# A two-layer hybrid decoder step on one core: evacuations, attention steps and weight parts are queued by the time their own engine gets to them, and low parts by DMA are chosen by an estimate of their landing

## The chip, the cores and the metric

One core of one Trainium2 chip runs the whole program. The metric is device microseconds of one execution; each time named as a median is over the runs taken, and one execution was also profiled. Engines are called as in the profile: PE (TensorE, its matmuls), PEld (its weight loads), DVE (VectorE), ACT (ScalarE), POOL (GpSimd), SP (SyncE). Transfers run on the 16 DMA engines of the core; SP, ACT and POOL issue them.

## The reference

Two layers over 576 tokens (512 of a prompt, 8 sequences of 8 sampled tokens), width 1024, all in float32:

```python
for l in range(DEPTH):
    rq, rk, rv, rg, sq, sk, sv, mq, g_r, g_s, g_m = in_proj(x, w_in[l], pos)
    ret_o = retention(rq, rk, rv); swa_o = sink_window_attend(sq, sk, sv)
    mem_o = mem_attend(mq, mk, mv)
    ret_b = (silu(rg) * group_norm(ret_o, gn_g)) @ w_br_ret
    swa_b, mem_b = swa_o @ w_br_swa, mem_o @ w_br_mem
    merged = sigmoid(g_r) * ret_b + sigmoid(g_s) * swa_b + sigmoid(g_m) * mem_b
    x = layer_norm(ALPHA * x + merged @ w_out, ln1_g, ln1_b)
    h = square(relu(x @ w_up))
    x = layer_norm(ALPHA * x + h @ w_down, ln2_g, ln2_b)
```

## The kernel before

**Tiling.** Features lie on the partitions. The tokens are two groups, A and B, of 288. A weight *unit* is a 1024x128 piece of a weight matrix, 128x1024 in the chip (512 KB); `unit_order` lists 154 of them a layer, in the order mk, mv (memory keys and values), rk, rq, rv, rg (retention), sv, sk, sq (window attention), gr and br, mq, gs and bs, gm and bm (gates and branch outputs), wo, up, then pairs ua/ub with dh, and dn. Every float32 value is held as two fp32r parts, high and low, and a product of a unit with a group is 24 matmuls of 128x288: 8 slots, each high by high, high by low and low by high.

**Parts of a unit.** The raw unit comes by a DMA that SP issues (`fetch`, 545). `split` (551) makes the two parts: the high part is a cast on ACT or DVE. The low part is made in one of two ways: on DVE, a subtraction of 128x1024 (`T<-T,T`); or by ACT and a DMA, where ACT writes minus the high part (ACTIVATE `T<-T`) and POOL issues a DMA that adds the raw unit to it (`T<-T` by POOLq). Lines 560 and 561 choose: the DMA is taken if the unit's use lies over `FAR` = 11 us ahead and its key is none of mq, gs, bs, gm, bm. The pairs ua/ub of the MLP are seven half-width products of sums of the two units (`block`, 570; `pair_steps`, 661), as in Strassen's scheme, and `sums` (713) forms the matching sums of tokens.

**The order of the work.** All instructions are written by one Python program in the order in which it calls them; each engine runs its own in that order. `Clock` (268) holds a cost model of every engine, which runs along while the program is written; it decides the order alone, and its times are no measurements. `plan` (240) gives every unit a planned time of use. `run` (617) writes the steps of a phase; inside a product, after each 6 matmuls, `Filler.advance` (404) looks at what else may be put in: generators (`add`), which yield tiles they wait for, and single instructions put off by `later` (390). Both are put in when `ok` (399) says that their input is ready `EARLY` = 0.4 us after the planned time of PE, or earlier. `tick` (598) puts in the parts of the next unit: all of them at once, when ACT has no work ahead or the use is within `LEAD` = 13 us. `soonest` (523) takes the engine that would be done first. Evacuations of a product (`up_ev`, the closure `evac` of `pair_steps`) are written right behind its last matmul.

**The layer norms.** `norm_ev` (842) is called on each of the 8 outputs of wo or dn for a group, adds it to the residual y, and keeps running sums. `shift` (867) subtracts a mean from y (`T<-T,u` 128x1152); `half` squares and sums; `last` (887) ends the norm: two mean products on PE (`pa<-t,ones`), reciprocal root in tiles `ln` and `u`, four multiplies of y (`z = [mult(i) ...]`, 939), the affine step on ACT (`T<-T,par` 128x288, which writes the high part of the next input) and an `end` on DVE that makes the low part. wo runs all of A, then all of B, then up all of A and all of B, so that A's norm ends under B's products of wo, and B's norm under A's products of up. The start of layer 1 does the same with dn and the first products, whose mk and mv units do not depend on the norm.

All instructions are recorded with line 359, the wrapper `timed`, so rows are told apart by tiles: `T` big tiles, `u` and `t` tiles of 128x288, `pg` and `pa` PSUM banks.

Of the kernel before, what the change touches and what calls it, by code (L numbers as in the profile page):

```python
# [8 lines left out]
F32 = mybir.dt.float32  # L9
# [27 lines left out]
EARLY = 0.4  # L37
EARLY_PE = -0.8
LEAD = 13.0
FAR = 11.0  # L40
DN_SKEW = 7
START = 3
STEP = 2
# [331 lines left out]
    pass  # L375


class Filler:
    def __init__(self, clock):
        self.t = 0.0  # L380
# [6 lines left out]
        self.gens.append([gen, self.clock.now, lane])  # L387
        self.gens.sort(key=lambda r: r[2])

    def later(self, fn, wait, *aps):  # L390
        self.late.append((self.t + wait, fn, aps))

    def flush(self, upto=None):
        due = [x for x in self.late if upto is None or x[0] <= upto or self.ok(x[2])]
        self.late = [x for x in self.late if x not in due]
        for _, f, _ in due:
            f()

    def ok(self, cond):
        if isinstance(cond, float):  # L400
            return cond <= self.clock.now
        return self.clock.ready(cond) - (EARLY_PE if isinstance(cond, Pe) else EARLY) <= self.clock.now

    def advance(self, dt):
        self.t += dt
# [31 lines left out]
                self.step(rec)  # L437

    def drain(self):
        self.flush()  # L440
        while self.gens:
            busy = set()
            for rec in list(self.gens):
                if rec[2] in busy:
                    continue
                busy.add(rec[2])
                self.step(rec)


class Builder:  # L450
    def __init__(self, nc, tc, I, O, coff, pools):
        self.tc, self.I, self.O, self.coff = tc, I, O, coff
        self.clock = Clock()
        self.nc = Engines(nc, self.clock)
        self.sb, self.ps, self.dr = pools
        self.n = 0
        self.fill = Filler(self.clock)
        self.banks = []
        self.raw, self.w = {}, {}
        self.dma_next = self.split_next = 0  # L460
        self.cap = 4
        self.items = items()
        self.item = {(k, b): i for i, (u, k, b) in enumerate(self.items)}
        self.use = plan(self.items)
        self.live = {}
        self.between = iter(())
        self.fill.tick = self.tick

# [82 lines left out]
    def split(self, i):  # L551
        u, k, b = self.items[i]
        if b is not None:
            self.w[i] = self.block(u, b)
            self.live[i] = 1
            return
        raw = self.raw.pop(u)
        hi = self.tile([P, 8, P], F32R)
        lo = self.tile([P, 8, P], F32R)
        if self.use[i] - self.fill.t > FAR and k[1] not in ("mq", "gs", "bs", "gm", "bm") and u > 15 \  # L560
                and (k[1] != "dh" or k[2] == 0):
            self.nc.scalar.copy(hi, raw)
            self.nc.scalar.activation(lo, raw, AF.Copy, scale=-1.0)
            self.nc.gpsimd.dma_start(lo, raw, accum_op=ALU.add)
        else:
            self.split_into(hi, lo, raw, True)
        self.w[i] = (hi, lo)
        self.live[i] = 2

    def block(self, u, b):  # L570


        V = self.nc.vector
        ra, rb = self.raw[u - 1], self.raw[u]
# [12 lines left out]
        w = self.tile([P, 8, P], F32R)  # L587
        self.nc.scalar.copy(w[:, 0:4], src)
        if b == 5 and self.items[self.split_next][1][2] == 7:
            self.nc.scalar.activation(w[:, 4:8], src, AF.Copy, scale=-1.0)  # L590
            self.nc.gpsimd.dma_start(w[:, 4:8], src, accum_op=ALU.add)
        else:
            V.tensor_tensor(w[:, 4:8], src, w[:, 0:4].bitcast(F32), ALU.subtract)
        if b == 6:
            del self.raw[u - 1], self.raw[u], self.raw[u, "s"]
        return w[:, 0:4], w[:, 4:8]

    def tick(self):
        n, i = len(self.use), self.split_next
        if i >= n or self.use[i] > self.fill.t + LOOK:  # L600
            return
# [15 lines left out]
    def run(self, steps, cap=3):  # L617
# [5 lines left out]
        for i, (units, fn, tick) in enumerate(steps):  # L623
            while units and self.split_next <= max(units):
                self.feed()
            fn()
            for u in units:
                if last[u] == i:
# [32 lines left out]
    def pair_steps(self, key, XT, evac):  # L661


        V, S = self.nc.vector, self.nc.scalar
# [15 lines left out]
        def sub(k, a, b):  # L680
            st[k] = self.u()
            V.tensor_tensor(st[k], a, b, ALU.subtract)

        def e0():
            st["s1"] = self.u()
            S.copy(st["s1"], st["z"])

        def e1():
            sub("w", st.pop("v"), st.pop("s1"))
# [3 lines left out]

        def e3():
            sub("o", st.pop("v7"), st["y"])
            evac(1, "B", st.pop("o"))

        def e4():
            evac(0, "A", st.pop("z"))

        def e5():
            sub("o", st["w"], st.pop("x"))
            evac(1, "A", st.pop("o"))

        def e6():
            sub("o", st.pop("y"), st.pop("w"))
            evac(0, "B", st.pop("o"))
        return [step(0, lambda: (bank("z", "g"), True, e0)), step(1, lambda: (bank("v", "g"), True, e1)),
                step(2, lambda: (bank("x", "a"), True, e2)), step(3, lambda: (bank("y", "a"), True, e3)),
                step(4, lambda: (st["z"], False, e4)), step(5, lambda: (st["x"], False, e5)),  # L710
                step(6, lambda: (st["y"], False, e6))]

# [129 lines left out]
    def norm_ev(self, g, y, l, gi, eps, out, scale=None, bias=1.0):  # L842
# [24 lines left out]
        def shift():  # L867
# [4 lines left out]
            V.tensor_scalar(st["c"], pm, 4.0, None, ALU.mult)  # L872
            cb = st["c"].unsqueeze(1).to_broadcast([P, 4, n])
            self.pick(y[1], st["c"], bias=bias).tensor_tensor(y[1], y[1], cb, ALU.subtract)

        def half():
            c = st.pop("c")
# [9 lines left out]
        def last():  # L887
# [48 lines left out]
            if out is not None:  # L936
                out[g]["h"] += [self.tile([P, 4, n], F32R) for _ in range(2)]
                out[g]["l"] += [self.tile([P, 4, n], F32R) for _ in range(2)]
            z = [mult(i) for i in range(4)]
            step = 1 if out is None else STEP  # L940
            wait = ()
            for i in range(0, 4, step):
# [22 lines left out]
        def ev(m, ps):  # L965
# [22 lines left out]
            elif m > 4:  # L988
# [4 lines left out]
                if m == 7:  # L993
                    self.fill.flush()
                    self.pick(sq, st["s2"]).tensor_tensor(st["s2"], st["s2"], sq, ALU.add)
                    st["last"] = last()
                    self.fill.add(st["last"], 0)
                else:
                    self.fill.later(lambda: self.pick(sq, st["s2"], bias=bias).tensor_tensor(st["s2"], st["s2"], sq, ALU.add),
# [481 lines left out]
    def layer(self, l, X):  # L1481
# [377 lines left out]
        for q in range(2, 8):  # L1859
            H.append(self.feat_tiles(1))  # L1860
            steps = []
            for j in range(2):
                def pev(i, g, ps, j=j, q=q):
                    up_ev(2 * j + i, H[-1])(g, ps)
# [7 lines left out]
            if 2 < q < 5:  # L1872
                k = ("swk", "swv")[q - 3]
                nc.gpsimd.dma_start(self.O[k + "_c"][l], self.I[k + "_n"][l])
        del Ts, XT, X1
        H = {g: {k: [h[g][k][0] for h in H] for k in "hl"} for g in "AB"}
        if True:
# [93 lines left out]
```

## Time and profile before

| | |
|---|---|
| median of 3 runs | 2158.07 us (2150.84 to 2158.13) |
| profiled execution | 2157.69 us, its span 2155.9 us |
| granted TensorE clock, mean of the span | 0.992 |
| PE busy | 2118.5 us, 98% |
| DVE, ACT, POOL busy | 59%, 43%, 11% |
| DMA | 292.42 MB, mean 136 GB/s |

A row of a group gives busy time, and behind a bar the idle time of the engine just before. In a timeline, a row is a run of like instructions on one engine: its start, its length from the first start to the last end, and in brackets how long the engine had stood idle before the first of them and what ended that. `pg<-T,T` is the output tile and its inputs. A run of matmuls that is longer than its count of matmuls times the time of one holds gaps too. For a DMA, "to landing" runs from its issue to its last byte.

### The profile page before, as it was taken

What the parts mean: (1) busy time and instruction counts of PE and PEld (TensorE: products, weight loads), DVE (VectorE), ACT (ScalarE), POOL (GpSimd) and SP (SyncE); (2) the same over time, 40 slices, a digit from 0 to 9 for tenths busy, and PEclk for the clock granted to TensorE, in tenths of its full rate; (3) what the DMA queues carried; (4) which work ended last, traced back from release to release, by engine and by line L of the source; (5) the groups of instructions that cost most, each with busy time, mean ns of one, the idle gap of its engine ahead of it and who ended that gap; (6) DMA issues with size and microseconds to landing.
All of it is one profiled execution on the core that took longest, in us unless ns stands there. A gap on an engine that the chain in (4) does not pass through costs nothing.

```text
span 2155.9 us, 39206 instructions
## 1 busy us (share of the span) xinstructions
PE 2118.5 (98%) x16180; PEld 2058.2 (95%) x16180; DVE 1261.5 (59%) x2705; ACT 925.6 (43%) x1750; POOL 232.9 (11%) x297
## 2 busy tenths in 40 slices
PE   9999999999999999999989999999999999999997
PEld 8999999999999999999989999999999999999997
DVE  6455644456547576765745556444565565767766
ACT  4333355322256444446553333562221665444452
POOL 0111111000022000000321111000000220000012
PEclk9999999999999999999999999999999999999999
DMA  8455645434375422225895556544342854222242
GB/s 316 114 143 134 166 118 120 145 109 144 119 211 127 126 94 84 79 88 151 204 266 143 144 141 174 122 114 132 135 157 85 229 120 130 79 79 99 98 122 60
DMA packets 87618, 292.42 MB, mean 136 GB/s; under 512 B 9552, under 2 KB 19280, under 8 KB 87376
## 3 DMA queue, kind: packets, MB, share of 16 engines
q0 software_dynamic: 31408, 113.79, 24.0%
q1 hardware_dynamic: 50944, 168.27, 22.8%
q10 hardware_dynamic: 5088, 7.87, 1.1%
q8 instruction: 127, 2.08, 0.4%
q14 instruction: 51, 0.42, 0.1%
HBM read 200.89 MB, written 15.99 MB: 101 GB/s over the span
## 4 chain that ended last, share of the span: by engine, by line
PE 91%; DVE 4%; issue 2%; DMA 2%; ACT 1%; POOL 0%; SPq 0%; DVEq 0%; POOLq 0%; ACTq 0%
PE pg L359 69%; PE pa L359 23%; DVE T L359 3%; DMA T<-T 1%; ACT T L359 1%; DVE u L359 0%; DMA T<-in_wall 0%; ACT u L359 0%; DMA T<-in_memT 0%; SPq L359 0%; DVE ln L359 0%; DVE accA L359 0%; DVE s L359 0%; POOL T L359 0%; POOL rc L359 0%
## 5 line engine op out<-in xcount | busy, mean ns | idle before, releaser
L359 PE MATMUL pg<-T,T 128*128 128x288 f32 (+1 forms) x11840 | 1643.3, 297 | 19.3 <-ACT T L359 10.9
L359 PEld LDWEIGHTS pg<-T,T 128*128 128x128 f32 x11840 | 1591.4, 190 | 44.4 <-ACT T L359 17.0
L359 PE MATMUL pa<-T,T 128*128 128x288 f32 (+8 forms) x3368 | 449.5, 303 | 2.4 <-DVE u L359 2.4
L359 ACT CAST T<-T 128x1024 fp32r<-128x1024 f32 (+6 forms) x464 | 354.6, 789 | 210.1 <-DVE T L359 174.7
L359 PEld LDWEIGHTS pa<-T,T 128*128 128x128 f32 (+3 forms) x3368 | 399.7, 176 | 23.0 <-issue 9.5
L359 DVE TENSOR_TENSOR T<-T,T 128x512 fp32r<-128x512 f32 (+8 forms) x418 | 361.9, 878 | 85.2 <-ACT T L359 75.4
L359 POOL DMA_DIRECT2D T<-T x145 | 124.7, 868 | 1379.2 <-ACT T L359 1013.2
L359 ACT ACTIVATE T<-T 128x1024 fp32r<-128x1024 f32 (+2 forms) x157 | 165.3, 1054 | 10.5 <-DVE T L359 8.2
L359 ACT ACTIVATE t<-pg 128x288 f32<-128x288 f32 x128 | 52.6, 411 | 215.8 <-PE pg L359 210.5
L359 ACT ACTIVATE u<-u 128x288 f32<-128x288 f32 x200 | 89.0, 445 | 96.0 <-DVE u L359 92.0
L359 DVE TENSOR_TENSOR T<-u,T 128x288 fp32r<-128x288 f32 x160 | 72.4, 454 | 78.0 <-ACT T L359 78.0
L359 ACT COPY T<-pg 128x512 f32<-128x512 f32 (+2 forms) x44 | 20.8, 479 | 213.0 <-PE pg L359 213.0
L359 DVE TENSOR_TENSOR T<-T,pg 128x288 f32<-128x288 f32 x128 | 57.7, 451 | 75.6 <-PE pg L359 75.1
L359 ACT CAST T<-u 128x288 fp32r<-128x288 f32 x160 | 69.3, 433 | 52.6 <-DVE u L359 48.6
L359 DVE TENSOR_TENSOR T<-T,u 128x288 f32<-128x288 f32 (+2 forms) x136 | 88.1, 660 | 3.8
L359 DVE SCALAR_TENSOR_TENSOR T<-t,pg 128x288 f32<-128x288 f32 x64 | 29.0, 453 | 94.0 <-ACT t L359 76.2
L359 DVE TENSOR_TENSOR T<-T,pa 128x288 f32<-128x288 f32 (+1 forms) x92 | 52.1, 567 | 25.1 <-PE pa L359 23.7
L359 DVE TENSOR_TENSOR T<-pa,T 128x512 fp32r<-128x512 f32 (+2 forms) x48 | 24.9, 533 | 64.9 <-ACT T L359 64.7
L359 DVE SCALAR_TENSOR_TENSOR u<-t,pg 128x288 f32<-128x288 f32 x64 | 28.8, 450 | 55.8 <-PE pg L359 55.2
L359 DVE TENSOR_TENSOR u<-u,pa 128x288 f32<-128x288 f32 x72 | 32.6, 453 | 35.2 <-PE pa L359 35.0
L359 ACT CAST T<-pa 128x512 fp32r<-128x512 f32 (+2 forms) x44 | 19.4, 451 | 70.2 <-PE pa L359 66.3
L359 DVE CAST T<-T 128x1024 fp32r<-128x1024 f32 (+1 forms) x71 | 45.2, 641 | 1.0 <-DMA T<-in_wall 1.0
(164 smaller groups left out, 1095.3 us busy)
## 6 DMA issues: line engine op xcount, KB each, us to landing
T<-in_wall SPq DMA_DIRECT2D x305, 512.0 KB, 4.2
T<-T POOLq DMA_DIRECT2D x141, 512.0 KB, 5.7
T<-in_mck POOLq DMA_DIRECT2D x16, 512.0 KB, 4.4
T<-in_mcv POOLq DMA_DIRECT2D x16, 512.0 KB, 6.6
T<-in_s POOLq DMA_DIRECT2D x8, 512.0 KB, 8.2
out_state_s<-T POOLq DMA_DIRECT2D x8, 512.0 KB, 3.8
T<-in_xT SPq DMA_DIRECT2D x4, 576.0 KB, 10.4
T<-in_xT ACTq DMA_DIRECT2D x4, 576.0 KB, 6.8
```

The source lines that it names most:

```text
L359: r = f(*a, **kw)
```

## The change

- `FAR` and the list of keys go. `in_time` estimates, with the cost model, when ACT would be done, when POOL would issue, and when the bytes would land behind the DMAs already put in, and takes the DMA way if that and `MARGIN` = 1.5 us lie before the use.
- The low part on DVE and the parts of a `block` become generators (`part`, `proceed`): each is put in when the model says its engine gets to it with its input ready, at the latest before the step that uses it.
- `ok` compares readiness no longer with PE's planned time alone, but with the later of that and the time at which the engine (`On`) is free.
- In `pair_steps` the copy of the first bank (`e0`) goes to the sooner of ACT and DVE, and three of four evacuations of a pair are put off by `later` for ACT.
- In `norm_ev`, A's four final multiplies wait in the program until B's shift has been put in (`shifting`).
- `settle` empties the put-off list at the end of the pairs and in `drain`.

```diff
-FAR = 11.0
+MARGIN = 1.5
...
+class On(tuple):
+    def __new__(cls, eng, *aps):
+        r = tuple.__new__(cls, aps)
+        r.eng = eng
+        return r
...
-    def later(self, fn, wait, *aps):
-        self.late.append((self.t + wait, fn, aps))
+    def later(self, fn, wait, *aps, eng="vector"):
+        self.late.append((self.t + wait, fn, On(eng, *aps)))
...
+    def settle(self):
+        while self.late:
+            self.flush()
+
     def ok(self, cond):
         if isinstance(cond, float):
             return cond <= self.clock.now
-        return self.clock.ready(cond) - (EARLY_PE if isinstance(cond, Pe) else EARLY) <= self.clock.now
+        c = self.clock
+        if isinstance(cond, Pe):
+            return c.ready(cond) - EARLY_PE <= c.now
+        return c.ready(cond) - EARLY <= max(c.now, c.te[cond.eng] if isinstance(cond, On)
+                                            else min(c.te["vector"], c.te["scalar"]))
...
         if b is not None:
-            self.w[i] = self.block(u, b)
+            w = self.tile([P, 8, P], F32R)
+            self.w[i] = w[:, 0:4], w[:, 4:8]
+            self.part(i, self.block(w, u, b))
...
-        if self.use[i] - self.fill.t > FAR and k[1] not in ("mq", "gs", "bs", "gm", "bm") and u > 15 \
-                and (k[1] != "dh" or k[2] == 0):
+        if u > 15 and (k[1] != "dh" or k[2] == 0) and self.in_time(i, raw):
             self.nc.scalar.copy(hi, raw)
             self.nc.scalar.activation(lo, raw, AF.Copy, scale=-1.0)
             self.nc.gpsimd.dma_start(lo, raw, accum_op=ALU.add)
         else:
-            self.split_into(hi, lo, raw, True)
+            def low(raw=raw):
+                self.rounded(hi, raw)
+                yield On("vector", hi)
+                self.nc.vector.tensor_tensor(lo, raw, hi.bitcast(F32), ALU.subtract)
+            self.part(i, low())
...
+    def in_time(self, i, src):
+        c, n = self.clock, src.free_size()
+        t = max(c.te["scalar"], c.ready((src,))) + 2 * (0.19 + n / 1200.0)
+        t = max(t, c.te["gpsimd"]) + 1.04
+        t = max(t + 1.7, c.te["dma"]) + n * P * 4 / 360e3 + 0.9
+        return t + MARGIN < c.now + self.use[i] - self.fill.t
+
+    def part(self, i, gen):
+        cond = next(gen, None)
+        if cond is not None:
+            self.parts[i] = [gen, cond]
+
+    def proceed(self, upto=None):
+        for i in list(self.parts):
+            gen, cond = self.parts[i]
+            while cond is not None and (i == upto or self.fill.ok(cond)):
+                cond = next(gen, None)
+            if cond is None:
+                del self.parts[i]
+            else:
+                self.parts[i][1] = cond
...
+        yield On("scalar", src)
         self.nc.scalar.copy(w[:, 0:4], src)
...
+            yield On("vector", w[:, 0:4])
             V.tensor_tensor(w[:, 4:8], src, w[:, 0:4].bitcast(F32), ALU.subtract)
...
     def tick(self):
+        self.proceed()
...
+            for u in units:
+                if u in self.parts:
+                    self.proceed(u)
             fn()
...
+        def later(i, g):
+            o = st.pop("o")
+            self.fill.later(lambda: evac(i, g, o), 4.0, o, eng="scalar")
+
         def e0():
             st["s1"] = self.u()
-            S.copy(st["s1"], st["z"])
+            e = self.soonest((("scalar", 0.0), ("vector", 0.2)), st["z"])
+            (e.copy if e is self.nc.scalar else e.tensor_copy)(st["s1"], st["z"])
...
             sub("o", st.pop("v7"), st["y"])
-            evac(1, "B", st.pop("o"))
+            later(1, "B")
...
             self.pick(y[1], st["c"], bias=bias).tensor_tensor(y[1], y[1], cb, ALU.subtract)
+            self.shifting = False
...
-            z = [mult(i) for i in range(4)]
+            z = []
+            for i in range(4):
+                while out is not None and g == "A" and self.shifting:
+                    yield 0.4
+                z.append(mult(i))
...
                     st["last"] = last()
+                    self.shifting = True
                     self.fill.add(st["last"], 0)
```

Where the instructions come to stand, at three places. The number behind a tile's letter only tells tiles apart, and differs between the two programs.

First place, layer 0, from wo into up. **ACT before**, evacuations of up's products of A (`u<-pg`, relu; `u<-u`, square; cast to `T`), then the affine steps of B's norm (`par`):

```order
L359 ACTIVATE u_7693<-pg_7668 128x288
L359 ACTIVATE u_7693<-u_7693 128x288
L359 CAST T_7436<-u_7693 128x288
L359 ACTIVATE u_7737<-pg_7698 128x288
L359 ACTIVATE u_7737<-u_7737 128x288
L359 CAST T_7436<-u_7737 128x288
L359 ACTIVATE T_7716<-T_6608,par_85 128x288 x4
L359 ACTIVATE T_7717<-T_6609,par_85 128x288 x4
L359 ACTIVATE u_7787<-pg_7761 128x288
```
**ACT now**, the same stretch:

```order
L359 ACTIVATE u_7665<-pg_7626 128x288
L359 ACTIVATE u_7665<-u_7665 128x288
L359 CAST T_7459<-u_7665 128x288
L359 ACTIVATE u_7695<-pg_7670 128x288
L359 ACTIVATE u_7695<-u_7695 128x288
L359 CAST T_7459<-u_7695 128x288
L359 ACTIVATE T_7637<-T_6627,par_85 128x288 x4
L359 ACTIVATE T_7638<-T_6628,par_85 128x288 x4
L359 ACTIVATE u_7745<-pg_7720 128x288
```
The affine steps of B stood behind all eight evacuations of A; they stand behind the sixth now.

**DVE before**, the end of A's reciprocal root (`ln`) and A's final multiplies (`T_6604`, `T_6605` with `u_7172`):

```order
L359 TENSOR_TENSOR ln_7194<-ln_7174 128x288
L359 SCALAR_TENSOR_TENSOR ln_7194<-ln_7194,u_7171 128x288
L359 SCALAR_TENSOR_TENSOR u_7172<-ln_7194,ln_7174 128x288
L359 TENSOR_TENSOR T_6604<-T_6604,u_7172 128x576 x2
L359 TENSOR_TENSOR T_6605<-T_6605,pa_7100 128x1152
L359 TENSOR_TENSOR T_6605<-T_6605,u_7172 128x576 x2
```
**DVE now**, where `T_6627` and `T_6628` are B's residual and `u_7308` its shift, `T_6623` is A's:

```order
L359 SCALAR_TENSOR_TENSOR T_6627<-T_6627,pg_7214 128x288
L359 TENSOR_TENSOR t_7275<-accB_7151,t_7274 128x288
L359 SCALAR_TENSOR_TENSOR T_6627<-T_6627,pg_7248 128x288
L359 TENSOR_SCALAR u_7308<-pa_7213 128x288
L359 TENSOR_TENSOR T_6628<-T_6628,u_7308 128x1152
L359 TENSOR_TENSOR T_6623<-T_6623,u_7191 128x576 x2
L359 TENSOR_TENSOR T_6624<-T_6624,pa_7119 128x1152
```
Right behind the root before; now behind two more additions of B's products and the subtraction of B's shift.

Second place, **ACT before** at the start of layer 1: COPY empties mk's banks (`pg`), and each CAST with ACTIVATE makes a unit's high part and the minuend of its low part by DMA:

```order
L359 COPY T_11939<-pg_11943 128x256
L359 CAST T_11995<-T_11915 128x1024
L359 ACTIVATE T_11996<-T_11915 128x1024
L359 COPY T_11939<-pg_11986 128x256
L359 CAST T_12036<-T_11960 128x1024
L359 ACTIVATE T_12037<-T_11960 128x1024
L359 COPY T_11939<-pg_12019 128x256
L359 CAST T_12075<-T_11993 128x1024
```
**ACT now**, the same banks:

```order
L359 CAST t_11975<-accB_11420 128x288
L359 CAST T_11992<-T_11819 128x1024
L359 COPY T_11979<-pg_11983 128x256
L359 COPY T_11979<-pg_12014 128x256
L359 CAST T_12056<-T_11990 128x1024
L359 ACTIVATE T_12057<-T_11990 128x1024
L359 COPY T_11979<-pg_12047 128x256
L359 CAST T_12095<-T_12021 128x1024
```
Of the units cast here, the first has no ACTIVATE behind it any more: the low parts of mk 3, mv 0, mv 1 and of one rv unit are DVE's now, and two copies of banks stand together.

Third place, **POOL before** in the middle of layer 0: loads of the cached keys and values (`in_`), with nothing between them:

```order
L359 DMA T_4380<-in_swk 128x1024
L359 DMA T_4382<-in_swv 128x1024
L359 DMA T_5004<-in_mck 128x1024
L359 DMA T_5006<-in_mck 128x1024
L359 DMA T_5160<-in_mck 128x1024
L359 DMA T_5162<-in_mck 128x1024
L359 DMA T_5280<-in_mcv 128x1024
```
**POOL now**:

```order
L359 DMA T_4381<-in_swk 128x1024
L359 DMA T_4383<-in_swv 128x1024
L359 DMA T_4446<-T_4251 128x1024
L359 DMA T_4519<-T_4301 128x1024
L359 DMA T_4640<-T_4443 128x1024
L359 DMA T_4701<-T_4516 128x1024
L359 DMA T_4760<-T_4637 128x1024
L359 DMA T_5010<-in_mck 128x1024
L359 DMA T_5012<-in_mck 128x1024
L359 DMA T_5090<-T_4896 128x1024
L359 DMA T_5167<-in_mck 128x1024
L359 DMA T_5169<-in_mck 128x1024
```
Five low parts by DMA (`T<-T`) stand ahead of the first load of cached memory keys, and single ones between the loads. Over both layers 41 low parts go from DVE to DMA, nearly all of mq, gs, bs, gm and bm, and 9 come back to DVE; 173 are by DMA where 141 were.

## Rows read from the trace of the kernel before

**Rows 1.** The page: busy time by engine; issues, KB, median us to landing.
```profile
PE 2118.5 (98%) x16180; PEld 2058.2 (95%) x16180; DVE 1261.5 (59%) x2705; ACT 925.6 (43%) x1750; POOL 232.9 (11%) x297
...
T<-T POOLq DMA_DIRECT2D x141, 512.0 KB, 5.7
```

**Rows 2.** Waits of PE: us in total, times, longest us.
```profile
PE pg L359 <- ACT T L359: 10.9, 7, 2.5
PE pg L359 <- DVE T L359: 3.4, 3, 2.1
PE pa L359 <- DVE u L359: 3.3, 4, 1.2
PE pg L359 <- DMA T<-T: 3.2, 2, 2.9
```

**Rows 3.** Stretches: length, busy us (x instructions) by engine, PEclk, DMA share, GB/s.
```profile
756.00:810.00 54.00, 54.00 (x407) 54.00 (x407) 38.20 (x68) 23.67 (x49) 0.00 (x0) 1.00 0.30 98
1080.00:1134.00 54.00, 47.69 (x312) 44.05 (x311) 21.10 (x46) 28.25 (x47) 13.38 (x19) 0.94 0.92 256
500.00:600.00 100.00, 99.52 (x810) 97.48 (x810) 57.82 (x117) 25.29 (x62) 4.62 (x8) 1.00 0.37 126
```

**Rows 4.** Timeline, `wo` into `up`, layer 0: start us, us, engine, operation [idle <-releaser].
```profile
653.19 1.43 DVE L359 TENSOR_TENSOR T<-T,u 128x576 f32<-128x576 f32 x2
...
660.15 1.36 DVE L359 TENSOR_TENSOR T<-T,u 128x1152 f32<-128x1152 f32 x1
...
677.43 0.46 DVE L359 TENSOR_TENSOR T<-u,T 128x288 fp32r<-128x288 f32 x1 [2.49 <-ACT T L359]
...
694.03 4.49 ACT L359 ACTIVATE T<-T,par 128x288 fp32r<-128x288 f32 x8
...
694.71 7.83 PE L359 MATMUL pg<-T,T 128*128 128x288 f32 x22 [1.97 <-ACT T L359]
...
702.92 1.32 PE L359 MATMUL pg<-T,T 128*128 128x288 f32 x8 [0.38 <-DVE T L359]
```

**Rows 5.** Timeline, `wo` into `up`, layer 1.
```profile
1764.84 9.35 PE L359 MATMUL pg<-T,T 128*128 128x288 f32 x39 [1.97 <-ACT T L359]
```

**Rows 6.** Timeline, last pair of layer 0 into `dn`.
```profile
1010.53 1.22 DVE L359 TENSOR_TENSOR T<-T,T 128x1024 fp32r<-128x1024 f32 x1
...
1012.17 3.46 PE L359 MATMUL pa<-T,T 128*128 128x288 f32 x24 [1.19 <-DVE u L359]
...
1017.29 0.40 PE L359 MATMUL pg<-T,T 128*128 128x288 f32 x1 [0.87 <-ACT T L359]
...
1018.57 13.42 PE L359 MATMUL pg<-T,T 128*128 128x288 f32 x95 [0.88 <-ACT T L359]
```

**Rows 7.** Timeline, start of layer 1.
```profile
1077.39 0.84 POOL L359 DMA_DIRECT2D T<-T  x1 [3.17 <-ACT T L359]
...
1085.68 1.22 PE L359 MATMUL pg<-T,T 128*128 128x512 f32 x2 [2.89 <-DMA T<-T]
...
1111.46 0.53 PE L359 MATMUL pg<-T,T 128*128 128x288 f32 x2 [2.06 <-DVE T L359]
...
1112.94 5.23 PE L359 MATMUL pg<-T,T 128*128 128x288 f32 x28 [0.95 <-DVE T L359]
```

**Rows 8.** Timeline, last pair of layer 1 into `dn`.
```profile
2080.94 3.45 PE L359 MATMUL pa<-T,T 128*128 128x288 f32 x24 [1.17 <-DVE u L359]
...
2087.74 5.50 PE L359 MATMUL pg<-T,T 128*128 128x288 f32 x28 [2.55 <-ACT T L359]
```

**Rows 9.** DMA, 1077 to 1134 us: queue; issues, KB, median us to landing.
```profile
q0 software_dynamic: 2696, 10.00, 71.1%
...
T<-T POOLq DMA_DIRECT2D x11, 512.0 KB, 11.0
```

**Rows 10.** POOL's instructions on tile T: ns of one, min/median/max.
```profile
L359 POOL DMA_DIRECT2D T<-T x145: 832/850/1290, 70.2 to 2103.2; - x145
```

**Rows 11.** DVE's low parts of whole units: busy us, mean ns, idle before.
```profile
L359 DVE TENSOR_TENSOR T<-T,T 128x1024 fp32r<-128x1024 f32 x122 | 150.1, 1233 | 19.2 <-ACT T L359 12.5 <-DMA T<-T 3.7 <-DVE T L359 0.5
```

More of the change, by code (lines that the diff above doesn't have):

```diff
@@ L439, in drain @@
     def drain(self):
-        self.flush()
+        self.settle()
         while self.gens:
@@ L465, in __init__ @@
         self.live = {}
+        self.parts = {}
+        self.shifting = False
         self.between = iter(())
@@ L565, in split, with block @@
         else:
-            self.split_into(hi, lo, raw, True)
+            def low(raw=raw):
[3 more added lines that the diff above has]
+            self.part(i, low())
         self.w[i] = (hi, lo)
         self.live[i] = 2
-    def block(self, u, b):
+    def in_time(self, i, src):
[17 more added lines that the diff above has]
+                self.parts[i][1] = cond
+    def block(self, w, u, b):
         V = self.nc.vector
+        key = self.items[self.split_next][1]
         ra, rb = self.raw[u - 1], self.raw[u]
@@ L586, in block @@
             if b else ra[:, 0:4]
-        w = self.tile([P, 8, P], F32R)
+        if b == 6:
+            del self.raw[u - 1], self.raw[u], self.raw[u, "s"]
+        yield On("scalar", src)
         self.nc.scalar.copy(w[:, 0:4], src)
-        if b == 5 and self.items[self.split_next][1][2] == 7:
+        if b == 5 and key[2] == 7:
             self.nc.scalar.activation(w[:, 4:8], src, AF.Copy, scale=-1.0)
@@ L592, in block @@
         else:
+            yield On("vector", w[:, 0:4])
             V.tensor_tensor(w[:, 4:8], src, w[:, 0:4].bitcast(F32), ALU.subtract)
-        if b == 6:
-            del self.raw[u - 1], self.raw[u], self.raw[u, "s"]
-        return w[:, 0:4], w[:, 4:8]
     def tick(self):
+        self.proceed()
         n, i = len(self.use), self.split_next
@@ L659, in both, with pair_steps @@
         return [self.mstep(u, g, X, evac, slots, tag, late) for g, tag in zip("AB", tags)]
-    def pair_steps(self, key, XT, evac):
+    def pair_steps(self, key, XT, evac, xbank="a"):
         V, S = self.nc.vector, self.nc.scalar
@@ L702, in e5 @@
             sub("o", st["w"], st.pop("x"))
-            evac(1, "A", st.pop("o"))
+            later(1, "A")
         def e6():
             sub("o", st.pop("y"), st.pop("w"))
-            evac(0, "B", st.pop("o"))
+            later(0, "B")
         return [step(0, lambda: (bank("z", "g"), True, e0)), step(1, lambda: (bank("v", "g"), True, e1)),
-                step(2, lambda: (bank("x", "a"), True, e2)), step(3, lambda: (bank("y", "a"), True, e3)),
+                step(2, lambda: (bank("x", xbank), True, e2)), step(3, lambda: (bank("y", "a"), True, e3)),
                 step(4, lambda: (st["z"], False, e4)), step(5, lambda: (st["x"], False, e5)),
@@ L874, in shift @@
             self.pick(y[1], st["c"], bias=bias).tensor_tensor(y[1], y[1], cb, ALU.subtract)
+            self.shifting = False
         def half():
@@ L1862, in layer, with pev @@
             for j in range(2):
-                def pev(i, g, ps, j=j, q=q):
-                    up_ev(2 * j + i, H[-1])(g, ps)
+                def pev(i, g, ps, j=j, h=H[-1]):
+                    up_ev(2 * j + i, h)(g, ps)
                 steps += self.pair_steps((l, "ua", q, j), XT, pev)
@@ L1874, in layer @@
                 nc.gpsimd.dma_start(self.O[k + "_c"][l], self.I[k + "_n"][l])
+        self.fill.settle()
         del Ts, XT, X1
```

## The prediction

> **What bounds the kernel now.** I read the page first: PE is busy 98% of the span [rows 1], so only what PE loses can be won, and no other engine's busy time counts by itself. Then the waits of PE: they name four kinds worth having, ACT's and DVE's tiles T, DVE's u, and a low part that came by DMA (3.2 us in 2 times) [rows 2]. Then stretches of the span: the pairs of the MLP run without a gap, 54.00 of 54 us for 407 matmuls, so a matmul costs 54.00/407 = 0.133 us there; the middle of the layer loses 0.48 us in 100; the start of layer 1 loses 54 - 47.69 = 6.3 us in 54, with the DMA engines at 0.92 and a granted clock of 0.94 [rows 3]. The loss thus sits where one phase hands over to the next, and the timelines of the handovers show how. Where PE is fed one tile at a time it does not "wait" by name, its run of matmuls is only longer than count times 0.133; I count that excess too.
>
> The sum is made against the profiled execution: 2157.7 us, 0.4 under the median of 2158.07. 0.5%, about what a measurement of this kernel can tell from no change, is 10.8 us: faster means under 2147.3, slower over 2168.9.
>
> **The change part by part.** PE's products, the matmuls and the bytes of weights stay. What moves is ACT, DVE and POOL.
>
> *wo into up, layer 0.* PE waits 1.97 us for the first affine step of B's norm; its next 22 matmuls take 7.83 us instead of 22 x 0.133 = 2.9, since ACT delivers the 8 affine tiles in 4.49 us behind an evacuation that itself waited for PE; then 0.38 us for DVE [rows 4]. Lost: 1.97 + 4.9 + 0.38 = 7.3. In the new order the affine steps stand behind the sixth of A's evacuations, not the eighth, and so does the chain ahead of them: two products earlier, 2 x 24 x 0.133 = 6.4 us, nearly the whole loss. DVE's idling ahead of a low part of A's products (2.49 us at 677.43, where ACT had weight casts in front) is what lets the chain move [rows 4]. Against that, A's last multiplies now wait for B's shift. They ran at 653.19, the shift at 660.15 [rows 4], 7 us later. The four `end` steps that lay between now come behind, which brings the shift forward some 3 us, so A's multiplies end about 4 us later than now. No row shows a wait at A's entry, so A has room, but not measured how much. Bounds: 0 (room enough) and 7.3 (A's entry becomes what B's is now). I take 2.2, since the first product of up asks for the low parts of its input last; and 0.6 left at B. Gain 7.3 - 2.8 = 4.5, bounds 0 and 7.3.
>
> *The same in layer 1.* 1.97 us and 9.35 - 39 x 0.133 = 4.2 [rows 5]: 6.1 lost, the same remainder of 2.8, gain 3.3 (0 to 6.1).
>
> *Last pair into dn, layer 0.* PE waits 1.19, 0.87 and 0.88 us [rows 6]. The first is for two u differences on DVE, behind a 1.22 us subtraction of a weight's low part, which itself stood behind a bank copy on ACT. The copy goes to DVE when that is sooner, and the low parts are put in by the time DVE gets to them: what PE needs next comes first. The other two are ACT's casts of the pair's outputs, with weight casts of 1.05 us between; the evacuations now go by ACT's own time. Of 2.9 us I take 2.3 (0 to 2.9); what is late next there is the low parts of dn by DMA.
>
> *Start of layer 1.* PE waits 2.89 us at 1085.68 for a low part whose DMA POOL had issued at 1077.39, 8.3 us before, in the crowded stretch [rows 7]; both waits of this kind make 3.2 [rows 2]. The low parts of mk 3, mv 0 and mv 1 go to DVE, which is busy 21.10 of 54 us there [rows 3]; a subtraction takes 1.23 [rows 11]; these 3.2 us should go. Then 2.06 and 0.95 us for B's low parts on DVE at the first products that need B [rows 7]. B's mean products came behind the 2.89 us wait, so its chain comes earlier with it, and ACT's second group of affine steps no longer has a cast and an ACTIVATE of a unit ahead (some 2.1 us). I take 5.0 of 6.2 (1.5 to 6.2).
>
> *Last pair into dn, layer 1.* 1.17 and 2.55 us, and 5.50 - 28 x 0.133 = 1.8 of pacing [rows 8]: 5.5. The evacuations go ahead of the casts, but a full subtraction still stands before the difference that PE wants: 2.5 (0 to 5.5).
>
> *Low parts by DMA.* 41 go from DVE to DMA, 9 back. DVE loses 32 x 1.23 = 39 us of work [rows 11], worth nothing where PE already runs 99.5 of 100 us [rows 3]. What they can cost is lateness. The software queue took 71.1% of 57 us for 10.00 MB, so a part of 0.52 MB takes 0.711 x 57 / 10.00 x 0.52 = 2.1 us of all 16 DMA engines [rows 9]. Some 19 of the added ones fall in 120 us of each layer's middle: 19 x 2.1 / 120 = 0.33 on top of 0.37 [rows 3]. That is 0.7, short of the 0.92 at which a part took 11.0 us to land [rows 9] instead of 5.7 [rows 1]. The estimate in the change gives a part 1.04 for POOL, then 1.7 + 0.52 MB / 360 GB/s + 0.9 = 4.1, and 1.5 of margin: 6.6 in all, enough for 5.7, 4.4 short of 11.0 unless its own queue covers it. Bounds: 32 x 3.2/141 = 0.7 us at the rate of late parts in the whole kernel [rows 1, 2], and 41 x 3.2/11 = 11.9 at the rate of the crowded stretch [rows 9]. Nearer to the lower: 1.6.
>
> An issue of this kind takes POOL 832 to 1290 ns, median 850, with DVE busy 59% of the span [rows 1, 10]: none was held up by more than 0.5 us, and 41 more of them are no load on an engine that is busy 11%. So I add nothing for POOL. A rule of the Trainium skill speaks against that: "SBUF — State Buffer", section "SBUF: two separate sides", says that POOL cannot write a DMA's descriptors while DVE holds the port that they share, so that a short transfer takes some five times as long beside a copy on DVE; by it the sum would be that of the rival "POOL held up" below, by the rows it is 2142, and I go by the rows.
>
> *Start of the kernel.* One weight cast of the first units goes from ACT to DVE, ahead of another unit's low part; 0 to 0.9 us, I take 0.4. The put-off evacuations of the pairs, with 54.00 of 54 busy, cost nothing as long as DVE (38.20 of 54) and ACT (23.67) keep that room [rows 3]; without it each of 24 pairs could lose a wait like that of [rows 6], 1.2 us.
>
> Sum: 4.5 + 3.3 + 2.3 + 5.0 + 2.5 - 1.6 - 0.4 = 15.6; 2157.7 - 15.6 = 2142.
>
> **The rivals.**
>
> *The stalls move.* For: every handover is a chain of PE, ACT and DVE in turn, and A's entry, the landing of dn's low parts and the last subtraction are each late next. Half of the 17.6 comes back: 2157.7 - 8.8 + 2 = 2151. Against: the order lists show B's chain two products earlier, and PE's waits are named after it.
>
> *Low parts land late, slower.* One mechanism: in the middle of the layers POOL's queue now holds trains of five low parts ahead of the cached memory loads, and each further part in a train lands 2.1 us later than the one before, while the planner counts 1.5. If every second one of the 41 comes late by the mean of the two waits seen, 1.6 us, that is 33 us: 2157.7 - 17.6 + 33 = 2173. It decides from the point where a part lands more than about 6.6 us after its issue, as at the start of layer 1. For: 11.0 us at 0.92 [rows 9]. Against: 0.37 now [rows 3], and most parts are put in well ahead of their use.
>
> *POOL held up.* An added issue starts only when DVE's subtraction of 1.23 us [rows 11] beside it is over, and the parts that are tight, 2 of 11 as in the crowded stretch, are late by it: 41 x 2/11 x 1.23 = 9.2, 2151. Against: the longest of 145 issues was 0.44 us over the median [rows 10]. [...]
>
> *It does not act.* The chains are bound by their own durations; what stands ahead of an instruction in its queue had been done by then. PE's waits stay within 2 us of what they are, and the cost of the low parts takes that: 2157. For: the affine steps follow one another with nothing between. Against: ACT's casts stand between in the rows cited.
>
> *All of it.* Every gap counted closes, with no new one: 7.3 + 6.1 + 2.9 + 6.2 + 5.5 = 28.0, 2130.
>
> **How the numbers follow.** Forecast 0.50 (2136 to 2148), stalls move 0.25 (2147 to 2156), late low parts 0.07, POOL held up 0.02, no effect 0.09, all of it 0.07. Faster by over 0.5%: nearly all of the first, a quarter of the second, all of the last: 0.48 + 0.06 + 0.07 = 0.61. Slower: 0.07. The rest, 0.32, is within. The range leaves out the late low parts and the far ends of both sides: 2131 to 2157.
>
> **What would show it.** Right: in the waits of PE, ACT T falls from 10.9 to about 4 and DMA T<-T to under 2; the start of layer 1 is busy about 52 of 54 us; the entry of B into up shows no run of 22 matmuls in 7.8 us; a new wait of 2 us for DVE or ACT stands at A's entry into up; low parts land after 6 to 8 us in the middle. Wrong: PE's wait for DMA T<-T grows past 5 us, or waits for DVE appear within the pairs, or A's entry costs what B's did. Then the time is above 2147.

## The result: slower by 1.1%, and the profile after

The changed kernel takes 2181.13 us in the median of 6 runs (2177.82 to 2184.5), the kernel before 2158.10: ratio 1.0113, 95% interval 1.0096 to 1.0131. The profiled execution took 2179.34 us, its span 2177.6, 21.7 over the span before. 2142 was forecast.

From the page after, busy time by engine, and issues with KB and median us to landing, as [rows 1]:

```profile
PE 2122.9 (97%) x16180; PEld 2063.2 (95%) x16180; DVE 1202.0 (55%) x2635; ACT 990.7 (45%) x1817; POOL 265.0 (12%) x332
...
T<-T POOLq DMA_DIRECT2D x173, 512.0 KB, 5.5
...
T<-in_mcv POOLq DMA_DIRECT2D x16, 512.0 KB, 9.0
```

DVE has 59 us less to do, 39 of them foreseen (32 subtractions); the rest is mostly casts that went to ACT, whose busy time grew by 65 us. Low parts land as fast as before, after 5.5 us. PE's busy time grew by 4.4 us with the same matmuls, so its idle time grew by 17.3. The waits of PE after, as [rows 2]:

```profile
PE pg L359 <- DVE T L359: 12.3, 11, 3.4
PE pa L359 <- DMA T<-in_swk: 11.2, 2, 5.7
PE pg L359 <- ACT T L359: 6.5, 3, 3.4
PE pa L359 <- DMA T<-in_mcv: 4.3, 5, 1.7
PE pa L359 <- DVE T L359: 2.8, 1, 2.8
PE pg L359 <- DMA T<-T: 1.5, 1, 1.5
```

PE hardly waits for the low parts by DMA themselves: 1.5 us, less than the 3.2 before. New are the load of the cached window keys (`T<-in_swk`), the load of the cached memory values (`T<-in_mcv`), and DVE. Stretches around roughly the same work, before and then after, with length, busy us (x instructions) of PE, PEld, DVE, ACT, POOL, then PEclk, DMA share and GB/s (window attention, two parts of the memory attention, wo into up, the start of layer 1):

```profile
380.00:425.00 45.00, 45.00 (x399) 42.03 (x398) 23.86 (x49) 15.45 (x37) 1.95 (x3) 1.00 0.53 157
470.00:515.00 45.00, 45.00 (x400) 43.02 (x398) 25.79 (x60) 11.03 (x27) 3.14 (x6) 1.00 0.40 141
530.00:575.00 45.00, 44.52 (x398) 42.74 (x397) 25.36 (x53) 11.28 (x24) 2.11 (x4) 1.00 0.44 152
640.00:720.00 80.00, 77.16 (x546) 74.91 (x546) 46.49 (x84) 53.54 (x95) 18.37 (x21) 0.96 0.53 125
1050.00:1130.00 80.00, 73.69 (x513) 70.03 (x512) 46.95 (x92) 47.45 (x77) 24.12 (x29) 0.96 0.93 251
```

```profile
380.00:430.00 50.00, 44.27 (x371) 41.23 (x370) 13.65 (x39) 18.83 (x40) 5.13 (x7) 0.90 0.59 157
470.00:515.00 45.00, 42.08 (x365) 39.40 (x364) 19.33 (x52) 13.09 (x33) 4.94 (x8) 0.96 0.51 156
540.00:585.00 45.00, 43.18 (x381) 40.56 (x381) 15.22 (x42) 18.21 (x29) 7.31 (x10) 1.00 0.78 217
640.00:720.00 80.00, 75.89 (x550) 74.69 (x549) 55.10 (x92) 46.46 (x82) 25.73 (x26) 0.98 0.53 123
1060.00:1130.00 70.00, 66.35 (x455) 63.97 (x454) 56.80 (x98) 42.69 (x72) 25.46 (x30) 0.95 0.79 233
```

Length minus busy is PE's idle time: none before and 5.73 us after in the window attention, none and 2.92 in the first part of the memory attention, 2.84 and 4.11 from wo into up, 6.31 and 3.65 at the start of layer 1. Layer 1 repeats it: PE's two waits for the window keys make 11.2 us, the longer one 5.7. So the loss stands where PE had lost nothing, in the middle of the layer.

**The window attention.** Timeline after:

```profile
392.47 0.85 POOL L359 DMA_DIRECT2D T<-T  x1 [5.81 <-ACT T L359]
...
397.59 0.55 POOL L359 DMA_DIRECT2D T<-in_swk  x1 [4.27 <-DVE u L359]
...
404.52 2.09 PE L359 MATMUL pa<-T,u 64*32 64x128 f32 x64 [5.73 <-DMA T<-in_swk]
```

and before, the same load and the same matmuls:

```profile
391.07 0.56 POOL L359 DMA_DIRECT2D T<-in_swk  x1 [4.79 <-PE pa L359]
...
398.34 1.31 PE L359 MATMUL pa<-T,u 64*32 64x128 f32 x64
```

Before, the load was issued 7.3 us ahead of PE. After, POOL was free at 393.3, yet the load went out at 397.59. In the compiled program the load's waits are three, and each is for a transfer that POOL issued; before, DVE and PE stood among them:

```
before
L359 DMA T_4380<-in_swk 128x1024 [waits DMASW0_49,DVE_49,PE_49]
after
L359 DMA T_4381<-in_swk 128x1024 [waits DMASW7_49,DMASW4_49,DMASW0_49]
```

The row names DVE's u as releaser, an inference, and none of the three. The big tiles take their places from a ring of 38. In the compiled program the load's tile T_4381 has the place of T_4159, and T_4159 is the raw unit that the low part directly ahead in POOL's queue reads (T_4304<-T_4159, issued at 392.47). That transfer landed after 4.5 us, at 397.0, and the load went out at 397.59. I call this a held place. It is not the whole wait: the load then took 6.8 us to land, where it took 3.8 before, with the DMA engines at 0.95. So it was 6.5 us late and landed 3.0 us slower, against 3.5 us of room that it had before.

**The memory attention** shows a held place at DVE:

```profile
479.38 0.88 POOL L359 DMA_DIRECT2D T<-T  x1 [7.42 <-ACT T L359]
...
484.11 0.69 DVE L359 TENSOR_TENSOR T<-pa,T 128x512 fp32r<-128x512 f32 x1 [6.25 <-DMA T<-T]
...
484.85 1.82 PE L359 MATMUL pa<-T,T 128*128 128x512 f32 x4 [2.83 <-DVE T L359]
```

DVE has its inputs, and waits 6.25 us for a transfer `T<-T`. In the compiled program the tile it writes, T_5172, has the place of T_4985, the raw unit of the low part issued at 479.38, which landed after 4.5 us, at 483.9. Behind DVE PE waits 2.83. Later, four loads of memory values stand in POOL's queue behind a low part:

```profile
547.38 0.88 POOL L359 DMA_DIRECT2D T<-T  x1 [15.39 <-PE pg L359]
...
547.94 2.44 POOL L359 DMA_DIRECT2D T<-in_mcv  x4
...
559.13 0.65 PE L359 MATMUL pa<-T,T 128*32 128x128 f32 x16 [1.20 <-DMA T<-in_mcv]
```

This is another mechanism, the order of POOL's queue: by the compiled program what the four loads wait for themselves had been done by about 545, for the first of them at 540.9, but the low part ahead of them waited for ACT's ACTIVATE, which ended at 547.1.

### The profile page after: what moved, and what is told of

The parts are those of the page before. It is cut to its first block, busy times and chain, and to the rows that moved or that the text cites. A ratio compares the mean times of both kernels' runs of the same rounds, so it can differ in the third digit from the quotient of the medians.

```text
span 2177.6 us, 39356 instructions
## 1 busy us (share of the span) xinstructions
PE 2122.9 (97%) x16180; PEld 2063.2 (95%) x16180; DVE 1202.0 (55%) x2635; ACT 990.7 (45%) x1817; POOL 265.0 (12%) x332
## 5 line engine op out<-in xcount | busy, mean ns | idle before, releaser
L359 ACT CAST T<-T 128x1024 fp32r<-128x1024 f32 (+6 forms) x503 | 391.8, 805 | 200.2 <-DVE T L359 158.8
L359 DVE TENSOR_TENSOR T<-T,T 128x512 fp32r<-128x512 f32 (+8 forms) x386 | 321.0, 856 | 50.7 <-ACT T L359 45.7
L359 POOL DMA_DIRECT2D T<-T x177 | 152.2, 860 | 1572.4 <-ACT T L359 1375.9
L359 ACT ACTIVATE T<-T 128x1024 fp32r<-128x1024 f32 (+2 forms) x189 | 199.2, 1054 | 18.9 <-DMA T<-T 11.4
L359 ACT COPY u<-pg 128x288 f32<-128x288 f32 (+1 forms) x34 | 13.3, 392 | 125.5 <-PE pg L359 125.5
L359 ACT CAST T<-pa 128x256 fp32r<-128x256 f32 (+2 forms) x39 | 16.7, 433 | 63.9 <-PE pa L359 57.9
```

The costliest lines, as they stand in the source:

```text
L359: r = f(*a, **kw)
```

## The experiments

Every experiment was timed against the kernel before on the same chip; over the groups of runs, on three chips, that kernel's median was 2157.1 to 2157.7 us. The names S, T, U, V of the theories are those of the expectations.

**1. The five keys back on DVE.**

```diff
-        if u > 15 and (k[1] != "dh" or k[2] == 0) and self.in_time(i, raw):
+        if u > 15 and (k[1] != "dh" or k[2] == 0) and k[1] not in ("mq", "gs", "bs", "gm", "bm") \
+                and self.in_time(i, raw):
```

> The change with one thing undone: mq, gs, bs, gm and bm make their low parts on DVE again (39 low parts by DMA fewer). Both theories on DMA low parts (S: a raw unit keeps its place in the tile ring until its DMA has landed, and the tile that gets the place next is written late; T: the added transfers crowd POOL's queue and the DMA engines) expect PE's waits for the cached loads and for DVE in the memory attention to go, 8.5 + 7.8 + 5.3 + 2.1 + 2.7 = 26 us: about 2155. Rival U (parts and evacuations put off until their engine gets to them are what is late) expects 2175 to 2185.

2150.24 us, ratio 0.9966 (0.9954 to 0.9978). Rival U falls: the five keys cost 2181.1 - 2150.2 = 31 us, and the rest of the change gives 7. PE's waits for the cached loads are gone; what remains stands at the handovers.

**2. The same traffic without the held place.**

```diff
             def low(raw=raw):
                 self.rounded(hi, raw)
+                if extra:
+                    self.nc.gpsimd.dma_start(self.dram([P, 8, P]), hi.bitcast(F32))
```

Here `extra` is set where a unit of the five keys would have gone by DMA.

> As the kernel before it in this list, but each low part that went back to DVE is replaced by a DMA from POOL of the same 512 KB out of the high part into memory outside, so POOL's queue and the transfers are nearly as many as in the change while no raw unit is held by a DMA. S expects the time of that kernel, about 2155 (within 5). T expects that of the change, 2176 to 2185.

2150.89 us, 0.9974 (0.9963 to 0.9985). 37 transfers of 512 KB stand in POOL's queue again, and the time is that of experiment 1 as far as can be told. The window attention of this kernel, with such a transfer (`d<-T`) directly ahead of the load:

```profile
389.06 0.56 POOL L359 DMA_DIRECT2D d<-T  x1 [3.32 <-ACT T L359]
...
392.74 0.54 POOL L359 DMA_DIRECT2D T<-in_swk  x1 [3.12 <-DVE T L359]
...
397.79 1.31 PE L359 MATMUL pa<-T,u 64*32 64x128 f32 x64
```

PE does not wait. So neither the places in POOL's queue nor the bytes are the bulk of it. The engines' time is less well tested: POOL's transfers, packets, MB and share of the 16 engines' span, in the change, in experiment 1 and here:

```profile
q0 software_dynamic: 36016, 130.57, 27.7%
...
q0 software_dynamic: 30400, 110.12, 22.8%
...
q0 software_dynamic: 35728, 129.52, 25.1%
```

The bytes are nearly all back, but only 2.3 of the 4.9 points of engine time: here a plain transfer of a tile to memory outside takes the engines less time than a low part, which adds. For the window attention experiment 5 closes this gap; for the memory attention it stays open.

**3. Without the wait for B's shift.** The two lines `while out is not None ...: yield 0.4` are taken out of the full change.

> The change without the wait of A's last multiplies for B's shift. If the wait is what makes PE lose 7.1 us at the entry into up in each layer: 2181 - 10 = 2171, with some of B's loss coming back. Rival (the handover costs the same wherever it stands): A's loss goes and B's 6 to 7 us return, 2179 to 2183.

2177.19 us, 1.0095 (1.0074 to 1.0115): 4 us less in the median, against 10 or 0, but its interval overlaps that of the change, so it can't be told from nothing. A's entry is rid of the wait, and a new one has come, for the sums of B's mean:

```profile
PE pa L359 <- DVE t L359: 8.8, 2, 4.8
```

**4. The choice by landing time alone,** put into the kernel before in place of lines 560 and 561.

> The kernel before with one part of the change alone: the choice of DMA low parts by the estimate of their landing. S and T: PE's waits for the cached loads and in the memory attention come alone, 2158 + 26 = 2184. U: 2158 within 5.

2198.69 us, 1.0195 (1.0175 to 1.0216): 41 us slower, more than the 26 foreseen. The largest waits are those for the cached loads, as S and T both have it:

```profile
PE pa L359 <- DMA T<-in_mcv: 13.6, 12, 2.9
PE pa L359 <- DMA T<-in_swk: 12.8, 2, 6.6
```

With the old order around it, the choice does more harm than in the full change; the other parts gave 17.5 us of it back.

**5. One unit.** In the full change mq 0 alone goes back to DVE, two units of 308.

```diff
-        if u > 15 and (k[1] != "dh" or k[2] == 0) and self.in_time(i, raw):
+        if u > 15 and (k[1] != "dh" or k[2] == 0) and k[1:3] != ("mq", 0) and self.in_time(i, raw):
```

> The change with one unit a layer, mq 0, made on DVE again. It is the unit whose low-part DMA stands directly ahead of the load of the cached window keys in POOL's queue. S: that load no longer needs the place of a unit that a DMA is still reading, so PE's two waits for it (11.2 us in all) go and nothing else changes: 2181 - 11 to 16, 2165 to 2170. Rival: another low part takes the place ahead of the load and the wait stays, 2178 to 2184.

2167.52 us, 1.0047 (1.0031 to 1.0063): 13.6 us from two low parts. The load now goes out at 393.24, and PE does not wait, though POOL's transfers still take 27.5% of the 16 engines' span:

```profile
393.24 0.55 POOL L359 DMA_DIRECT2D T<-in_swk  x1 [7.04 <-DVE T L359]
...
398.25 1.31 PE L359 MATMUL pa<-T,u 64*32 64x128 f32 x64
```

**6. Traffic and ACT's pass.** Experiment 2 with `self.nc.scalar.copy(hi, hi.bitcast(F32))` ahead of each added transfer. There are 41 of them, and DVE's subtraction of the unit now stands behind ACT's pass too.

> The kernel with DVE low parts for mq, gs, bs, gm, bm and a DMA of the same size beside each, and now also one more pass of ACT over the 128x1024 high part per unit, as the DMA way costs ACT. What is still missing of the change's DMA way is only that the raw unit is held until the DMA lands. S: 2151, within 4. Rival V (ACT's second pass of 1.05 us per unit is what makes things late): 2165 or more.

2159.51 us, 1.0012 (1.0000 to 1.0023): between the two, 8.6 us over experiment 2. The waits for the window keys and for DVE in the memory attention stay away; the one for the memory values is back:

```profile
PE pa L359 <- DMA T<-in_mcv: 5.8, 7, 1.7
```

The row ahead of those loads shows what stood in their way:

```profile
533.01 0.54 POOL L359 DMA_DIRECT2D d<-T  x1 [15.51 <-ACT T L359]
...
533.54 1.04 POOL L359 DMA_DIRECT2D T<-in_mcv  x2
```

POOL's queue stood 15.5 us before a transfer that waited for ACT, and the loads left right behind it, as in the full change. So for the memory values the queue does matter, once ACT is later. How much of it is ACT's time, POOL's queue or the added transfers wasn't separated.

The traces also tell where the time goes: count the matmuls from the start, and compare when each profiled execution reaches the same one. Lost against the kernel before, in us, in both layers together:

| | window attention | memory attention |
|---|---|---|
| the change | 17.0 | 10.1 |
| experiment 2 | 0.2 | -0.9 |
| experiment 5 | 0.0 | 13.5 |
| experiment 6 | 0.1 | 9.1 |

In the window attention the loss comes and goes with the held place, and two low parts are enough for it. In the memory attention a loss of that size comes without any held place, from ACT's pass and the transfers; the held place at 484.11 is one wait there, and what its share would be on its own is not shown.

**7 to 9. What gives the 7 us.** From experiment 1 three things were undone, one at a time: the wait for B's shift (as in 3); the new `pair_steps` (copy on ACT, evacuations written at once); the putting off of parts (`part` runs its generator to the end).

> The kernel with the five keys on DVE again, and without the wait for B's shift. From the pair of runs with and without that wait in the full change: 4 us faster, 2146. If the entry into up costs PE 7 us either way: 2150, within 2.

2149.38 us, 0.9969 (0.9958 to 0.9979): no difference from experiment 1 that can be told.

> The kernel with the five keys on DVE again, and pair_steps as before (copy on ACT, evacuations written at once). If the forecast's mechanism for the last pair into dn holds, PE's waits for u and for ACT's casts come back there, 2.3 + 2.5 us: 2155. Rival (weight parts put off until DVE gets to them did it): 2150, within 2.

2147.50 us, 0.9959 (0.9947 to 0.9971): the interval overlaps that of experiment 1, so the new pair steps give nothing that can be told.

> The kernel with the five keys on DVE again, and all parts of a unit put in at once, as before (nothing put off until DVE or ACT gets to it). If putting off the low parts on DVE gives what this kernel has over the kernel before (7 us): 2157. Rival (the choice by landing time gives it, at the start of layer 1): 2150, within 2.

2151.58 us, 0.9970 (0.9959 to 0.9980): nor does putting the parts off.

**10. The old rule of lead.** Experiment 1 with `self.use[i] - self.fill.t > 11.0` for `in_time`.

> The kernel with the five keys on DVE again, and the DMA way chosen by the 11 us of lead as before, all else of the change kept. If the choice by landing time gives the 7 us, by the units of the start of layer 1 that went back to DVE (3.2 us of waits for a low part): 2153 to 2157. Rival (putting off gives it): 2150, within 2.

2159.48 us, 1.0011 (1.0002 to 1.0020). The 7 us are gone, all of them: in this order of the rest they hang on the landing estimate. At the start of layer 1 of this kernel a low part comes 7.6 us late:

```profile
1116.97 5.28 PE L359 MATMUL pg<-T,T 128*128 128x256 f32 x30 [7.59 <-DMA T<-T]
```

**11. A version from these runs,** experiment 1 without the new pair steps and without the wait for the shift.

> A version from the runs so far: the change without DMA low parts for the five keys, without the new pair_steps, and without the wait for B's shift. What is left is the putting off of weight parts and the choice by landing time. If undoing the last two adds up: 2147.5 - 0.9 = 2146.6, within 2; ahead of both kernels by over 0.4%. If they do not, 2150.

2149.28 us, 0.9961 (0.9948 to 0.9975): faster than both kernels, but the two don't add up.

**12. The landing estimate in the kernel before, the five keys on DVE.**

> The kernel before with one thing changed: where its DMA way was chosen by 11 us of lead, it is chosen by the estimate of the landing; the five keys stay on DVE, and nothing is put off, deferred or made to wait. If the landing estimate alone is what the good versions have over the kernel before: 2158 - 9 = 2149, within 3. Rival (it only serves in the new order of the rest): 2155 to 2160.

2154.21 us, 0.9987 (0.9975 to 0.9999): 3 us of the 9. The estimate needs the new order to be worth 7, and the new order is worth nothing without the estimate; which part of the new order it needs wasn't found. The lowest median is that of the version without the new pair steps, 2147.50, and its interval overlaps those of experiments 1, 2, 7, 9 and 11.

## Why the prediction was wrong, step by step

**Low parts by DMA: the step that failed.** "What they can cost is lateness", I wrote, and bounded the cost by late low parts, 0.7 to 11.9 us, taking 1.6. PE hardly waited for the parts (1.5 us; 5.5 us to landing). The cost of the five keys was 31 us, at other tiles. A low part by DMA reads the raw unit until it has landed, where DVE is through with it after 1.23 us, and the tile that gets the raw unit's place next can't be written. In the window attention that tile was a load in front of PE: 17.0 us in the two layers, and experiments 2, 5 and 6 each have the loss gone with the held place. The order lists showed low parts ahead of the cached loads, but not that two tiles share a place. The kernel's own cost model keeps its times by a tile's name, and so cannot know it either.

The term had a second hole: ACT's work. The DMA way takes an ACTIVATE of 1.06 us for each unit, and 37 casts went from DVE to ACT besides; ACT's busy time grew by 65 us, which the sum put at nothing. With one more pass of ACT beside 41 plain transfers the memory attention lost 9.1 us (experiment 6), about what the change lost there, 10.1, since a low part that waits for ACT keeps the loads behind it in POOL's queue. What the held places add in the memory attention stays open.

**The rival "low parts land late"** named the stretch, the trains ahead of the cached loads and the sign, and its 2173 is nearest to the result. That nearness is luck: its mechanism, late low parts, isn't what happened. What it had on its side was a reason to ask what else stands behind a transfer that waits.

**POOL held up.** The row after is 832/848/1256 ns for 177 issues:

```profile
L359 POOL DMA_DIRECT2D T<-T x177: 832/848/1256, 70.6 to 2123.4; - x177
```

The rule of the Trainium skill, "SBUF — State Buffer", section "SBUF: two separate sides", again does not show at these issues; leaving it out of the sum was right. The section tells the rule for copies on DVE, and the rival set it to subtractions, so these rows are a weak test of it; but two issues beside a cast of 128x1024 on DVE took 0.84 us as well (at 701.42 and 1038.13).

**wo into up.** B's own loss went, as forecast: its entry now runs without a gap (the last row below, 205 x 0.133 = 27.3). A's entry was priced at 2.2 us, on the reason that the order "brings the shift forward some 3 us". It did not come forward:

```profile
665.60 0.46 DVE L359 SCALAR_TENSOR_TENSOR u<-ln,ln 128x288 f32<-128x288 f32 x1
...
671.51 0.43 PE L359 MATMUL pa<-t,ones 128*128 128x288 f32 x2
...
671.97 0.46 DVE L359 TENSOR_SCALAR u<-pa 128x288 f32<-128x288 f32 x1 [1.41 <-PE pa L359]
...
687.39 0.53 PE L359 MATMUL pg<-T,T 128*128 128x288 f32 x2 [1.02 <-DVE T L359]
...
689.84 0.53 PE L359 MATMUL pg<-T,T 128*128 128x288 f32 x2 [1.91 <-DVE T L359]
...
691.31 3.92 PE L359 MATMUL pg<-T,T 128*128 128x288 f32 x16 [0.94 <-DVE T L359]
...
697.72 27.48 PE L359 MATMUL pg<-T,T 128*128 128x288 f32 x205
```

A's root was ready at 666.1. B's shift hung not on DVE, as I had it, but on B's mean product on PE, which stood in PE's queue until 671.51; its `u` follows at 671.97, A's multiplies after it. The low parts of A's input then make PE wait 1.02, 1.91 and 0.94 us. With the excess of the short runs, 0.27 twice and 3.92 - 16 x 0.133 = 1.8, A's entry loses 6.2 us where 2.2 was forecast and B's had lost 7.3 before: of the gain of 4.5 about 1 is left (0.5 in the table below). That A's entry costs what B's did was a sign of being wrong in the prediction. Experiment 3 shows a stall at B's sums in place of A's: the rival "the stalls move" described this place.

**Start of layer 1.** The 3.2 us for a low part went, as forecast, with the units on DVE. Of the 5.0 us 4.0 came in all, 2.7 of them idle time (6.31 to 3.65): a wait for DVE took the place of the others.

```profile
1091.42 8.68 PE L359 MATMUL pg<-T,T 128*128 128x256 f32 x48 [3.41 <-DVE T L359]
```

That it hangs on the landing estimate is shown by experiment 10; experiment 12 shows that the estimate does not give it alone.

**The pairs into dn.** 2.3 and 2.5 us were forecast, from the copy and the put-off evacuations, and 2.4 and 1.9 came. But the version without the new pair steps (experiments 7 to 9) is not slower, so the reason falls and the agreement is luck; what else shortened them wasn't tried.

**The sum.** Term by term, the time between the same two matmuls in the two profiled executions, to some 0.2 us:

| stretch, in us of the kernel before | forecast | measured |
|---|---|---|
| window attention, 363.6 to 455.7 and 1436.1 to 1534.7 | no loss named | 8.9 and 8.1 lost |
| memory attention, 455.7 to 632.5 and 1534.7 to 1691.7 | no loss named | 7.3 and 2.8 lost |
| wo into up, 632.5 to 893.3 and 1691.7 to 1897.9 | 4.5 and 3.3 gained | 0.5 gained, 0.9 lost |
| last pair into dn, 893.3 to 1051.6 and 1897.9 to 2097.3 | 2.3 and 2.5 gained | 2.4 and 1.9 gained |
| start of layer 1, 1051.6 to 1161.6 | 5.0 gained | 4.0 gained |

Without the failed step the rest of the change gives 7 us (experiment 1), not the 17.6 - 0.4 = 17.2 of the other terms. Most of what is missing is wo into up, where the stall taken out at B came back at A.

## What to carry to other kernels

When an instruction is moved from an engine to a DMA, count how long its *source* is held, and ask which tile gets that place next and who stands behind its first writer; the time to landing is only half of the price. A cost model that sets an order must know the places of a ring, not only the tiles' names. An engine that gets the work instead, here ACT, must be priced where others wait for it. And a change of several parts is best priced by the part that touches stretches where nothing was lost: here the parts aimed at the handovers moved 7 us, and the one that touched a stretch at 100% cost 31.

## What was not expected of the hardware

A wait costs more than its length. Length, busy us (x instructions) by engine, PEclk, DMA share, GB/s, after, around PE's wait of 5.73 us for the window keys:

```profile
390.00:398.00 8.00, 8.00 (x57) 6.46 (x56) 2.25 (x5) 3.01 (x5) 1.27 (x2) 1.00 0.55 137
398.00:404.50 6.50, 0.78 (x6) 0.56 (x6) 0.00 (x0) 2.30 (x3) 1.57 (x3) 0.75 0.95 305
404.50:412.00 7.50, 7.48 (x88) 7.44 (x89) 2.29 (x6) 3.50 (x11) 0.00 (x0) 0.53 0.53 122
412.00:420.00 8.00, 8.00 (x64) 7.95 (x62) 3.22 (x12) 1.34 (x3) 0.96 (x1) 1.00 0.61 160
```

PE ran without a gap at a granted clock of 1.00 until 398; then it stood for most of 6.5 us, and in the next 7.5 us the clock granted was 0.53, close to the lower of its two levels (1.2 and 2.4 GHz), with PE busy throughout. After that it was 1.00 again. At 0.53 the 7.5 us hold the work of some 0.53 x 7.5 = 4 us at full clock, so an estimate of 3.5 us comes on top of the wait. Counted between the same matmuls, the window attention of layer 0 lost 8.9 us with 5.73 of idle time: 3.1 on top. That fits PE's busy time having grown by 4.4 us with the same matmuls.

The four loads of memory values show another cost of standing together. In POOL's queue they left within 2.44 us, between two low parts, and over the kernel the median to landing of such loads rose from the 6.6 us of the page before to 9.0. "DMA: Bandwidth & Descriptors" of the Trainium skill, section "Issuing engines are not separate DMA queues", says that transfers share the same 16 engines and interleave whatever engine issued them; the trace agrees in so far as these loads landed slower in a stretch with a DMA share of 0.78 instead of 0.44.
